# A column mean over 8192 x 8192: whole-tile first load, deeper input buffering, an uneven cast split, one PSUM accumulator and a piecewise last tile

## The chip, the cores and the metric

The kernel runs on one core of a Trainium2 chip. The metric is the device time of one execution in microseconds (us). Beside it stands the span, which the profiler takes from the first to the last instruction of one execution; here it is about 1.8 us shorter than the time.

Engines in the profile: PE is the matmul engine and PEld its weight loads, DVE the vector engine, ACT the scalar engine, SP the engine that issues the DMAs (SPq is its queue). A DMA has landed when all of its bytes are in. The PE clock is the share of full speed that was granted to PE.

## The reference

```python
x = np.random.randn(8192, 8192).astype(np.float32)
def reference(x):
    return np.mean(x, axis=0)          # 8192 column means
```

The input has 268.4 MB, the output 32 KB. Every input byte has to come in from HBM once, and little arithmetic is done on it.

## The kernel before

The rows are taken in 64 tiles of 128 rows (4.19 MB each). A tile t is loaded in f32, cast to f16 as th by ACT (left half) and DVE (right half), and PE sums over its 128 rows by a matmul whose weight is a column of 1/8192. The 16 column chunks of 512 go to eight PSUM banks, two rows in each. Three buffers hold t, three hold th.

```python
STREAM_BUFS = 3
CAST_BUFS = 3
SPLIT_FIRST_DMA = True
SPLIT_LAST_DMA = True
# ... (w0, w1: 128x2 weights, 1/R in one column, 0 in the other)
for i in range(n_tiles):
    t = stream.tile([P, C], f32, tag="t")
    th = casts.tile([P, C], f16, tag="th")
    src = x[i * P : (i + 1) * P, :]
    if first and SPLIT_FIRST_DMA:
        for r0 in range(0, P, 32):                      # four DMAs of 32 rows
            nc.sync.dma_start(out=t[r0 : r0 + 32, :], in_=src[r0 : r0 + 32, :])
    elif last and SPLIT_LAST_DMA:                       # two DMAs of half the columns
        nc.sync.dma_start(out=t[:, 0:half], in_=src[:, 0:half])
        nc.sync.dma_start(out=t[:, half:C], in_=src[:, half:C])
    else:
        nc.sync.dma_start(out=t, in_=src)
    if not last:
        nc.scalar.copy(out=th[:, 0:half], in_=t[:, 0:half])
        nc.vector.tensor_copy(out=th[:, half:C], in_=t[:, half:C])
        # ... 16 matmuls
        continue
    # ... last tile: casts, 16 matmuls, eight copies 2x512 from PSUM by DVE and ACT in turn
nc.sync.dma_start(out=out[0:half], in_=stage[0:1, 0:half])
nc.sync.dma_start(out=out[half:C], in_=stage[1:2, 0:half])
```

## Time and profile before

| | before |
|---|---|
| time, median | 646.23 us (646.15 to 646.82, 4 runs) |
| span of the profiled run | 644.4 us |
| first cast starts (tile 0 has landed) | 23.3 us |
| from the first cast of tile 0 to the last full tile's (62 periods) | 603.6 us |
| from there to the end (the tail) | 17.5 us |

The first view is the page of the kernel before: busy time of each engine with its share of the span, the DMA engines' busy tenths and the rate moved in 40 equal slices of 16.1 us, the chain of waits that ended last by engine, and the two casting groups (busy us, mean ns of one, then the idle time before them and what ended it).

```profile
PE 358.3 (56%) x1024; PEld 110.7 (17%) x1024; DVE 148.4 (23%) x72; ACT 236.0 (37%) x70; POOL 0.2 (0%) x4
...
DMA  9999999999999999999999999999999999999994
GB/s 197 350 429 423 430 443 427 427 431 438 427 429 435 430 428 429 441 425 429 426 443 429 426 431 436 429 431 435 429 430 429 437 429 430 427 437 433 427 424 182
...
DMA 85%; ACT 12%; PE 1%; DVE 0%; SPq 0%; issue 0%; ACTq 0%; DVEq 0%
...
L78 ACT CAST th<-t 128x4096 f16<-128x4096 f32 x63 | 227.1, 3605 | 378.8 <-DMA t<-in_x_dram 360.4
L79 DVE CAST th<-t 128x4096 f16<-128x4096 f32 x63 | 144.5, 2294 | 483.7 <-DMA t<-in_x_dram 461.5
```

No compute engine is busy for more than 56% of the span, the chain is 85% DMA, and both casts spend their idle time waiting for t. This is a kernel bound by its input stream. But the two rows of slices disagree at the left edge: the DMA engines count as busy there, while the rate is 197 and 350 GB/s instead of about 430. So the busy share alone does not tell at what rate a DMA engine moves bytes. Windows of 5 us over the start make it plain (columns: window and its length, busy time and count on PE, PEld, DVE, ACT, POOL, then the PE clock, the DMA share and GB/s):

```profile
0.00:5.00 5.00, 0.00 (x0) 0.08 (x1) 0.15 (x4) 0.00 (x0) 0.20 (x4) 1.00 0.94 210
5.00:10.00 5.00, 0.00 (x0) 0.00 (x0) 0.00 (x0) 0.00 (x0) 0.00 (x0) 1.00 1.02 210
...
15.00:20.00 5.00, 0.00 (x0) 0.00 (x0) 0.00 (x0) 0.00 (x0) 0.00 (x0) 1.00 1.02 210
```

For 20 us the rate is 210 GB/s at a DMA share of about one. The DVE timeline shows what it costs (start, duration, engine, line, operation; in brackets the idle time before it and what ended it):

```profile
23.33 2.29 DVE L79 CAST th<-t 128x4096 f16<-128x4096 f32 x1 [22.38 <-DMA t<-in_x_dram]
32.95 2.29 DVE L79 CAST th<-t 128x4096 f16<-128x4096 f32 x1 [7.33 <-DMA t<-in_x_dram]
42.66 2.29 DVE L79 CAST th<-t 128x4096 f16<-128x4096 f32 x1 [7.41 <-DMA t<-in_x_dram]
```

Tile 0 takes 23.3 us to arrive, tile 1 only 9.6 us more, and from there the casts start 9.71 us apart, which is 4.19 MB / 9.71 us = 432 GB/s.

The other end is the tail, after the last full tile is in (timeline of the kernel before):

```profile
626.90 3.60 ACT L78 CAST th<-t 128x4096 f16<-128x4096 f32 x1 [6.11 <-DMA t<-in_x_dram]
...
630.55 7.04 PE L53 MATMUL psum_all<-th,w 128*2 128x512 f16 x24 [4.42 <-ACT th L78]
...
632.05 3.60 ACT L86 CAST th<-t 128x4096 f16<-128x4096 f32 x1 [1.54 <-DMA t<-in_x_dram]
...
636.78 1.90 ACT L89 CAST th<-t 128x2048 f16<-128x2048 f32 x1 [1.13 <-DMA t<-in_x_dram]
...
638.58 2.47 DVE L95 COPY stage<-psum_all 2x512 f32<-2x512 f32 x4 [0.47 <-PE psum_all L53]
...
641.48 0.25 SPq L100 DMA_DIRECT2D out_dram<-stage  x1
```

The second half of the last tile lands just before 636.78. Two casts, eight matmuls, eight small copies and two output DMAs follow, until the span ends at 644.4.

### The profile page before, as it was taken

How to read it: one execution, taken by the hardware profiler on the slowest of the kernel's cores; microseconds unless marked ns; L12 is line 12 of the kernel's file. 1: busy time of each engine (PE TensorE's matmuls, PEld its weight loads, DVE VectorE, ACT ScalarE, POOL GpSimd, SP SyncE). 2: the span in 40 equal slices, each digit the busy share in tenths (PEclk: the TensorE clock that was granted, in tenths of full speed). 3: DMA queues.
4: the chain of work that ended last, by engine and by line, in shares of the span. 5: the costliest groups of instructions: out<-in, count | busy, mean ns of one | idle time of the engine just before them, and what ended most of it. 6: DMA issues, size and time to landing. Idle time of an engine off the chain costs nothing.

```text
span 644.4 us, 2618 instructions
## 1 busy us (share of the span) xinstructions
PE 358.3 (56%) x1024; PEld 110.7 (17%) x1024; DVE 148.4 (23%) x72; ACT 236.0 (37%) x70; POOL 0.2 (0%) x4
## 2 busy tenths in 40 slices
PE   0256746547547546566457456556556466466455
PEld 0011211112112112112112112112112112111111
DVE  0122121221221221221221221221221221221222
ACT  0343342442442442442432432433433433433436
POOL 0000000000000000000000000000000000000000
PEclk9986678876786687677776886786677766876888
DMA  9999999999999999999999999999999999999994
GB/s 197 350 429 423 430 443 427 427 431 438 427 429 435 430 428 429 441 425 429 426 443 429 426 431 436 429 431 435 429 430 429 437 429 430 427 437 433 427 424 182
DMA packets 9425, 268.64 MB, mean 417 GB/s; under 512 B 1090, under 2 KB 1090, under 8 KB 1090
## 3 DMA queue, kind: packets, MB, share of 16 engines
q1 hardware_dynamic: 9412, 268.47, 98.5%
q8 instruction: 8, 0.13, 0.1%
q14 instruction: 5, 0.04, 0.0%
HBM read 268.44 MB, written 0.03 MB: 417 GB/s over the span
## 4 chain that ended last, share of the span: by engine, by line
DMA 85%; ACT 12%; PE 1%; DVE 0%; SPq 0%; issue 0%; ACTq 0%; DVEq 0%
DMA t<-in_x_dram 85%; ACT th L78 12%; PE psum_all L53 1%; DVE stage L95 0%; SPq L70 0%; DVE th L90 0%; ACTq L78 0%; DVEq L126 0%; SPq L75 0%; SPq L72 0%; DVEq L90 0%
## 5 line engine op out<-in xcount | busy, mean ns | idle before, releaser
L53 PE MATMUL psum_all<-th,w 128*2 128x512 f16 x1024 | 358.3, 527 | 281.7 <-ACT th L78 281.2
L78 ACT CAST th<-t 128x4096 f16<-128x4096 f32 x63 | 227.1, 3605 | 378.8 <-DMA t<-in_x_dram 360.4
L79 DVE CAST th<-t 128x4096 f16<-128x4096 f32 x63 | 144.5, 2294 | 483.7 <-DMA t<-in_x_dram 461.5
L53 PEld LDWEIGHTS <-w 128*2 128x2 f16 x1024 | 110.7, 108 | 528.8 <-issue 484.6
L78 ACT ACT_TABLE_LOAD x1 | 1.3, 1283 | 23.3 <-DMA t<-in_x_dram 23.3
L86 ACT CAST th<-t 128x4096 f16<-128x4096 f32 x1 | 3.6, 3604 | 1.5 <-DMA t<-in_x_dram 1.5
L90 DVE CAST th<-t 128x2048 f16<-128x2048 f32 x1 | 1.2, 1226 | 7.7 <-DMA t<-in_x_dram 7.7
L95 DVE COPY stage<-psum_all 2x512 f32<-2x512 f32 x4 | 2.5, 672 | 0.5 <-PE psum_all L53 0.5
L89 ACT CAST th<-t 128x2048 f16<-128x2048 f32 x1 | 1.9, 1899 | 1.1 <-DMA t<-in_x_dram 1.1
L97 ACT COPY stage<-psum_all 2x512 f32<-2x512 f32 x4 | 2.1, 572 | 0.2
L41 DVE MEMSET w<- 128x1 f16 x1 | 0.1, 59 | 0.8 <-PEq L115 0.8
L115 POOL MEMSET const-bfloat16-1.0<- 128x1 bf16 x1 | 0.1, 102 | 0.0
L115 POOL MEMSET const-uint8-127<- 128x1 uint8 x1 | 0.1, 102 | 0.0
L115 POOL MEMSET const-float32-0.0<- 128x1 f32 x1 | 0.1, 99 | 0.2 <-issue 0.2
L115 POOL MEMSET const-float32-1.0<- 128x1 f32 x1 | 0.1, 99 | 0.0
L42 DVE MEMSET w<- 128x1 f16 x1 | 0.1, 59 | 0.0
L44 DVE MEMSET w<- 128x1 f16 x1 | 0.1, 59 | 0.0
L45 DVE MEMSET w<- 128x1 f16 x1 | 0.1, 59 | 0.0
## 6 DMA issues: line engine op xcount, KB each, us to landing
t<-in_x_dram SPq DMA_DIRECT2D x62, 4096.0 KB, 25.4
t<-in_x_dram SPq DMA_DIRECT2D x4, 1024.0 KB, 14.4
t<-in_x_dram SPq DMA_DIRECT2D x2, 2048.0 KB, 23.1
out_dram<-stage SPq DMA_DIRECT2D x2, 16.0 KB
```

The source lines that it names most:

```text
L41: nc.vector.memset(w0[:, 0:1], inv)
L42: nc.vector.memset(w0[:, 1:2], 0.0)
L44: nc.vector.memset(w1[:, 0:1], 0.0)
L53: nc.tensor.matmul(out=psum_all[0:2, b * 512 : (b + 1) * 512], lhsT=ws[m], rhs=th[:, j : j + 512], start=start, stop=stop,)
L78: nc.scalar.copy(out=th[:, 0:half], in_=t[:, 0:half])
L79: nc.vector.tensor_copy(out=th[:, half:C], in_=t[:, half:C])
L86: nc.scalar.copy(out=th[:, 0:half], in_=t[:, 0:half])
L89: nc.scalar.copy(out=th[:, half : half + qtr], in_=t[:, half : half + qtr])
L90: nc.vector.tensor_copy(out=th[:, half + qtr : C], in_=t[:, half + qtr : C])
L95: nc.vector.tensor_copy(out=stage[sl], in_=psum_all[sl])
L97: nc.scalar.copy(out=stage[sl], in_=psum_all[sl])
L115: nc = _bacc.Bacc("TRN2", target_bir_lowering=False, num_devices=1)
```

## The change

It is a retuning of the whole kernel: the first tile comes in one DMA of 128 rows; four stream buffers and two cast buffers instead of three and three; ACT casts 6 of the 16 column chunks and DVE 10; each chunk c has its own 128x16 weight with 1/8192 in column c, so all 1024 matmuls accumulate into one 16x512 region of one bank; the last tile comes in pieces of 5, 5, 5 and 1 chunks and is cast chunk by chunk; one copy and one output DMA end it. (A branch with REBAL_ROWS is switched off by its zero.)

```diff
-STREAM_BUFS = 3
-CAST_BUFS = 3
-SPLIT_FIRST_DMA = True
-SPLIT_LAST_DMA = True
+STREAM_BUFS = 4
+CAST_BUFS = 2
+ACT_CHUNKS = 6
+REBAL_TILE = 30
+REBAL_ROWS = 0
+PIECE_CHUNKS = (5, 5, 5, 1)
 ...
+    wall = consts.tile([P, n_chunk * n_chunk], f16)
+    nc.vector.memset(wall, 0.0)
+    for c in range(n_chunk):
+        nc.vector.memset(wall[:, c * n_chunk + c : c * n_chunk + c + 1], inv)
 ...
         nc.tensor.matmul(
-            out=psum_all[0:2, b * 512 : (b + 1) * 512],
-            lhsT=ws[m],
-            rhs=th[:, j : j + 512],
+            out=acc[0:n_chunk, :],
+            lhsT=wall[:, c * n_chunk : (c + 1) * n_chunk],
+            rhs=th[0:P, c * chunk : (c + 1) * chunk],
 ...
-        if first and SPLIT_FIRST_DMA:
-            for r0 in range(0, P, 32):
-                nc.sync.dma_start(out=t[r0 : r0 + 32, :], in_=src[r0 : r0 + 32, :])
+            nc.sync.dma_start(out=t[:, :], in_=x[r0 : r0 + P, :])
+        cast(t, th, 0, ACT_CHUNKS, on_act=True)
+        cast(t, th, ACT_CHUNKS, n_chunk, on_act=False)
+        for c in range(n_chunk):
+            mm(th, c)
 ... (last tile)
+    for cpp in PIECE_CHUNKS:
+        nc.sync.dma_start(out=t[:, c0 * chunk : (c0 + cpp) * chunk], in_=...)
+        for k in range(cpp):
+            cast(t, th, c0 + k, c0 + k + 1, on_act=(k < cpp // 2))
+        for k in range(cpp):
+            mm(th, c0 + k, stop=...)
+        c0 += cpp
 ...
+    nc.vector.tensor_copy(out=stage[:, :], in_=acc[0:n_chunk, :])
+    nc.sync.dma_start(out=out_v, in_=stage[:, :])
```

More of the change, by code (lines that the diff above doesn't have):

```diff
@@ L25 @@
     R, C = x.shape
-    assert R % P == 0
-    n_tiles = R // P
-    inv = 1.0 / float(R)
-    n_bank = (C + 1023) // 1024
-    assert n_bank <= 8 and C == n_bank * 1024
-    half = C // 2
-    qtr = half // 2
+    n_chunk = 16
+    chunk = C // n_chunk
+    n_bank = n_chunk // 2
+    assert C == 8192 and R % P == 0
+    inv = 1.0 / float(R)
+    n_tiles = R // P
+    assert sum(PIECE_CHUNKS) == n_chunk
     stream = ctx.enter_context(tc.tile_pool(name="stream", bufs=STREAM_BUFS))
@@ L38 @@
     psum = ctx.enter_context(tc.tile_pool(name="psum", bufs=1, space=bass.MemoryType.PSUM))
-    w0 = consts.tile([P, 2], f16)
-    nc.vector.memset(w0[:, 0:1], inv)
-    nc.vector.memset(w0[:, 1:2], 0.0)
-    w1 = consts.tile([P, 2], f16)
-    nc.vector.memset(w1[:, 0:1], 0.0)
-    nc.vector.memset(w1[:, 1:2], inv)
-    ws = (w0, w1)
-    stage = consts.tile([2, half], f32)
-    psum_all = psum.tile([P, 512 * n_bank], f32)
-    def mm(th, m, b, start, stop):
-        j = m * half + b * 512
+    wall = consts.tile([P, n_chunk * n_chunk], f16)
@@ L53, in mm @@
+    nc.vector.memset(wall, 0.0)
+    for c in range(n_chunk):
+        nc.vector.memset(wall[:, c * n_chunk + c : c * n_chunk + c + 1], inv)
+    stage = consts.tile([n_chunk, chunk], f32)
+    acc = psum.tile([P, chunk], f32)
+    out_v = out.rearrange("(c j) -> c j", j=chunk)
+    started = [False]
+    def mm(th, c, stop=False):
+        st = not started[0]
+        started[0] = True
         nc.tensor.matmul(
-            out=psum_all[0:2, b * 512 : (b + 1) * 512],
-            lhsT=ws[m],
@@ L56, in mm, with cast @@
-            rhs=th[:, j : j + 512],
-            start=start,
+            out=acc[0:n_chunk, :],
+            lhsT=wall[:, c * n_chunk : (c + 1) * n_chunk],
+            rhs=th[0:P, c * chunk : (c + 1) * chunk],
+            start=st,
             stop=stop,
         )
-    for i in range(n_tiles):
-        first = i == 0
-        last = i == n_tiles - 1
+    def cast(t, th, c0, c1, on_act):
+        sl = (slice(0, P), slice(c0 * chunk, c1 * chunk))
+        if on_act:
+            nc.scalar.copy(out=th[sl], in_=t[sl])
+        else:
+            nc.vector.tensor_copy(out=th[sl], in_=t[sl])
@@ L64 @@
+    for i in range(n_tiles - 1):
+        r0 = i * P
         t = stream.tile([P, C], f32, tag="t")
         th = casts.tile([P, C], f16, tag="th")
-        src = x[i * P : (i + 1) * P, :]
-        if first and SPLIT_FIRST_DMA:
-            for r0 in range(0, P, 32):
-                nc.sync.dma_start(out=t[r0 : r0 + 32, :], in_=src[r0 : r0 + 32, :])
-        elif last and SPLIT_LAST_DMA:
-            nc.sync.dma_start(out=t[:, 0:half], in_=src[:, 0:half])
-            nc.sync.dma_start(out=t[:, half:C], in_=src[:, half:C])
-        else:
-            nc.sync.dma_start(out=t, in_=src)
@@ L77 @@
-        if not last:
-            nc.scalar.copy(out=th[:, 0:half], in_=t[:, 0:half])
-            nc.vector.tensor_copy(out=th[:, half:C], in_=t[:, half:C])
-            for b in range(n_bank):
-                mm(th, 0, b, first, False)
-            for b in range(n_bank):
-                mm(th, 1, b, False, False)
-            continue
-        nc.scalar.copy(out=th[:, 0:half], in_=t[:, 0:half])
-        for b in range(n_bank):
-            mm(th, 0, b, first, False)
-        nc.scalar.copy(out=th[:, half : half + qtr], in_=t[:, half : half + qtr])
@@ L90 @@
-        nc.vector.tensor_copy(out=th[:, half + qtr : C], in_=t[:, half + qtr : C])
-        for b in range(n_bank):
-            mm(th, 1, b, False, True)
-            sl = (slice(0, 2), slice(b * 512, (b + 1) * 512))
-            if b % 2 == 0:
-                nc.vector.tensor_copy(out=stage[sl], in_=psum_all[sl])
-            else:
-                nc.scalar.copy(out=stage[sl], in_=psum_all[sl])
-    nc.sync.dma_start(out=out[0:half], in_=stage[0:1, 0:half])
-    nc.sync.dma_start(out=out[half:C], in_=stage[1:2, 0:half])
+        if i == REBAL_TILE and REBAL_ROWS:
+            q = REBAL_ROWS
+            nc.scalar.dma_start(out=t[0:q, :], in_=x[r0 : r0 + q, :])
+            nc.scalar.dma_start(out=t[q:P, :], in_=x[r0 + q : r0 + P, :])
+        else:
+            nc.sync.dma_start(out=t[:, :], in_=x[r0 : r0 + P, :])
@@ new lines @@
+        cast(t, th, 0, ACT_CHUNKS, on_act=True)
+        cast(t, th, ACT_CHUNKS, n_chunk, on_act=False)
+        for c in range(n_chunk):
+            mm(th, c)
+    r0 = (n_tiles - 1) * P
+    src = x[r0 : r0 + P, :]
+    t = stream.tile([P, C], f32, tag="t")
+    th = casts.tile([P, C], f16, tag="th")
+    c0 = 0
+    for cpp in PIECE_CHUNKS:
+        nc.sync.dma_start(
+            out=t[:, c0 * chunk : (c0 + cpp) * chunk],
+            in_=src[:, c0 * chunk : (c0 + cpp) * chunk],
+        )
+        for k in range(cpp):
+            cast(t, th, c0 + k, c0 + k + 1, on_act=(k < cpp // 2))
+        for k in range(cpp):
+            c = c0 + k
+            mm(th, c, stop=c == n_chunk - 1)
+        c0 += cpp
```

## The prediction

> **What bounds it now.** The input stream. The page's 40 slices show the DMA engines 9 tenths busy or more in every slice but the last, PE 56%, ACT 37%, DVE 23%; the chain of waits is 85% DMA of t and 12% ACT cast (the cast is only the link that frees a stream buffer; two other tiles are queued meanwhile). In the timeline the DVE casts start 9.71 us apart, 4.19 MB each, 432 GB/s. [...] So in steady state neither a fourth stream buffer, nor the 6/10 cast split, nor one PSUM accumulator can gain anything.
>
> **Where time is left.** (a) Start. The first cast waits until 23.3 us, but tile 1 follows only 9.65 us later. Windows of 1 us show zeros near 5, 10, 15 and 20 us: each of the four 32-row pieces of tile 0 takes about 5.05 us for 1 MB, 208 GB/s, though the slices call the engines busy. [...] half rate, as measured. (b) Tail. The last half tile lands at 636.76; two casts, 8 matmuls, eight 2x512 copies and two output DMAs follow until 644.4: 7.6 us.
>
> **What the change does.**
> - First tile as one 128-row DMA: 20.2 us of transfer becomes 9.7, so the first casts start at about 12.8 us instead of 23.3. On the critical path: -10.5 us (estimate from the above).
> - Middle: 62 periods unchanged. The cast becomes 2.7 us ACT / 2.9 DVE (estimate, scaling 3.605 us for 4096 columns on ACT, 2.294 on DVE) instead of 3.6. Off the path: 0. PE: the same 1024 matmuls of 512 columns, at most 6.8 us a tile[...]. CAST_BUFS 2 is enough: cast plus matmuls end 9.7 us after landing, the buffer is wanted after 19.4.
> - Last tile in 5/5/5/1 chunks: the last piece lands about 0.6 us after the third. The third piece's casts hold DVE about 1.4 us, then the last cast 0.43 (estimates from 2.29 and 1.23 us for 4096 and 2048 columns), then matmuls, one 16x512 copy (0.67) and one output DMA instead of two. I expect 5.8 us (full clock) to 6.8 us (half clock) after the last landing, instead of 7.6: -0.9 to -1.8. [...]
> - Seventeen memsets on idle DVE in the first 2 us: 0.
>
> **Sum.** 646.2 - 10.5 - 1.4 + 0.2 = 634.5; I say 634.2 us, range 632.6 to 636.2. The 2% line is at about 633.4, so it is close: faster 0.33, same 0.65, slower 0.02.
>
> **What shows each step.** First cast near 12.8 us, second about 9.7 later; the first two slices (197 and 350 GB/s) become near 400 and 430. Cast period stays 9.71. ACT busy falls to about 180 us and DVE rises to about 190, with no gain from it. From last landing to end about 6 us. PE busy about the same.
>
> **What would make it wrong.** The half-rate start may be a cold start and not the row split: then the first cast stays late and the time is near 644. Accumulating every matmul into one bank could stall PE enough to hold cast buffers: the waits view would show DVE waiting for PE and the period over 9.71. [...] One period of 10.98 us (near 80 us) is a hiccup of 1.3 us that may come or not.

The sum came to 634.5 us, and its -10.5 and -1.4 stand above with where they come from. Its + 0.2 is a guess for the narrow pieces; without it the sum is 634.3. That no buffer, split or accumulator could gain in steady state rests on the DMA's share alone (85% of the chain of waits, 90% busy or more in all slices but the last); that the stream could not be faster was not shown. The 6.8 us of matmuls a tile are an estimate from the trace before: in its slow stretches the weight loads start 0.43 us apart, and 16 matmuls took 6.50 us.

## More of the kernel before

Every run quoted was in the fast state. A program on one core has no second die to compare with, so only the spread of its own runs can show that.

## The result, and the profile after

The changed kernel took 633.91 us (median of 8 runs, 633.58 to 634.49), the kernel before 646.35 us in the same rounds (13 runs, 646.07 to 646.82). The ratio is 0.9808, with a 95% interval of 0.9798 to 0.9818: 1.9% faster, with the line of 2% inside the interval. All ratios here are the mean time of one kernel's fast runs over that of the other's fast runs of the same rounds, so they are not quite the ratio of the medians.

The span fell by 644.4 - 632.2 = 12.2 us. Read from the DVE timelines, it divides so:

| stretch | before | after | difference | predicted |
|---|---|---|---|---|
| start, to the first cast | 23.33 | 13.02 | -10.3 | -10.5 |
| first cast to the last full tile's, 62 periods | 603.6 | 604.2 | +0.6 | 0 |
| tail, from there to the end | 17.5 | 15.0 | -2.5 | -1.4 + 0.2 |

The page after (engines, and the rate in the 40 slices):

```profile
PE 360.0 (57%) x1024; PEld 118.6 (19%) x1024; DVE 182.9 (29%) x91; ACT 178.1 (28%) x70; POOL 0.2 (0%) x4
...
GB/s 373 433 437 431 432 431 433 433 431 430 432 433 431 432 428 433 431 431 431 428 433 431 431 432 430 431 435 431 431 430 431 431 433 430 431 431 430 431 418 234
```

The two slow slices have gone (373 and 433 GB/s). ACT lost 58 us of busy time and DVE gained 34; as the stream is the limit, this shows nowhere in the middle. The windows over the start:

```profile
0.00:5.00 5.00, 0.00 (x0) 0.09 (x1) 0.49 (x17) 1.28 (x1) 0.20 (x4) 1.00 0.69 242
5.00:10.00 5.00, 0.00 (x0) 0.00 (x0) 0.00 (x0) 0.00 (x0) 0.00 (x0) 1.00 1.05 452
```

The DVE timeline over the start:

```profile
13.02 2.83 DVE L69 CAST th<-t 128x5120 f16<-128x5120 f32 x1 [11.62 <-DMA t<-in_x_dram]
22.71 2.83 DVE L69 CAST th<-t 128x5120 f16<-128x5120 f32 x1 [6.87 <-DMA t<-in_x_dram]
```

The first tile is in at 13.0 us, and the next follows 9.7 us later as before. The +0.6 us in the middle is a few odd periods (one of 11.24 us at tile 6, where the kernel before had 10.98, and one of 10.09 near the end); in the other runs the same stretch took from 603.7 to 604.4 us, so no part of the change can be read from it (a_rows32_tile30, which slows the stream there on purpose, and a_earlype, whose last cast is cut, are left out).

The tail after:

```profile
617.18 2.75 ACT L67 CAST th<-t 128x3072 f16<-128x3072 f32 x1 [6.98 <-DMA t<-in_x_dram]
...
619.99 8.79 PE L56 MATMUL acc<-th,wall 128*16 128x512 f16 x32 [4.43 <-ACT th L67]
...
626.35 1.14 ACT L67 CAST th<-t 128x512 f16<-128x512 f32 x2 [1.94 <-DMA t<-in_x_dram]
626.35 1.43 DVE L69 CAST th<-t 128x512 f16<-128x512 f32 x4 [1.98 <-DMA t<-in_x_dram]
...
628.82 0.68 DVE L103 COPY stage<-acc 16x512 f32<-16x512 f32 x1 [1.03 <-PE acc L56]
629.52 0.36 SPq L104 DMA_DIRECT2D out_dram<-stage  x1
```

The line to look at is the second one. PE ran 32 matmuls as one unbroken group, all of the last full tile's and all of the last tile's, and the final copy waited for the end of it. The clock granted to PE moved during that group (windows after; the PE clock is the third number from the end):

```profile
620.00:622.00 2.00, 2.00 (x7) 0.72 (x7) 1.12 (x4) 1.14 (x2) 0.00 (x0) 0.65 1.00 420
622.00:624.00 2.00, 2.00 (x6) 0.59 (x5) 0.73 (x3) 0.73 (x2) 0.00 (x0) 0.50 0.98 409
624.00:626.00 2.00, 2.00 (x11) 0.82 (x10) 0.37 (x2) 0.41 (x1) 0.00 (x0) 1.00 0.60 236
626.00:628.80 2.80, 2.78 (x13) 0.97 (x11) 1.43 (x4) 1.14 (x2) 0.00 (x0) 1.00 0.02 6
```

In two windows of 2 us with a clock of 0.65 and 0.50 there are 7 and 6 matmuls, in the next one at 1.00 there are 11. Finer windows of this trace (0.1 us) put the half clock at 620.6 to 624.0 us, 3.4 us long.

How much this matters shows in seven profiled runs whose code from the last full tile on is the same (the changed kernel and six experiments of the next section that alter only how tile 0 or tile 30 is loaded):

| profiled runs | half clock around the group | group of 32 matmuls | tail |
|---|---|---|---|
| changed kernel, a_rows32, a_rows64, a_cols4 | 3.3 to 3.4 us | 8.8 us | 14.8 to 15.0 us |
| a_rows64_mid, a_rows32_strided, a_rows32_tile30 | 6.7 to 6.8 us | 9.9 to 10.0 us | 15.9 to 16.1 us |

The pages show it more coarsely: the clock of the last of the 40 slices is 8 tenths in the first four and 7 tenths in the other three.

Where the half clock is twice as long, the group and the tail are about 1.1 us longer with the same code. Tails of different kernels have to be compared at the same length of half clock, and the -2.5 us of the table above belongs to the short one (in the kernel before it was 3.4 us too). No run here tells what sets its length.

### The profile page after: what moved, and what is told of

The parts are those of the page before. It is cut to its first block, busy times and chain, and to the rows that moved or that the text cites. A ratio compares the mean times of both kernels' runs of the same rounds, so it can differ in the third digit from the quotient of the medians.

```text
span 632.2 us, 2631 instructions
## 1 busy us (share of the span) xinstructions
PE 360.0 (57%) x1024; PEld 118.6 (19%) x1024; DVE 182.9 (29%) x91; ACT 178.1 (28%) x70; POOL 0.2 (0%) x4
## 4 chain that ended last, share of the span: by engine, by line
DMA 90%; DVE 7%; PE 1%; ACT 0%; issue 0%; SPq 0%; DVEq 0%; ACTq 0%
DMA t<-in_x_dram 90%; DVE th L69 7%; PE acc L56 1%; ACT th L67 0%; SPq L80 0%; DVEq L69 0%; DVE stage L103 0%; ACTq L67 0%
## 5 line engine op out<-in xcount | busy, mean ns | idle before, releaser
L56 PE MATMUL acc<-th,wall 128*16 128x512 f16 x1024 | 360.0, 529 | 268.7 <-ACT th L67 268.7
L69 DVE CAST th<-t 128x5120 f16<-128x5120 f32 (+1 forms) x73 | 181.7, 2497 | 444.7 <-DMA t<-in_x_dram 444.7
L67 ACT CAST th<-t 128x3072 f16<-128x3072 f32 (+1 forms) x69 | 176.8, 2566 | 448.7 <-DMA t<-in_x_dram 448.7
L56 PEld LDWEIGHTS <-wall 128*16 128x16 f16 x1024 | 118.6, 116 | 509.7 <-issue 467.6
## 6 DMA issues: line engine op xcount, KB each, us to landing
t<-in_x_dram SPq DMA_DIRECT2D x1, 256.0 KB, 34.7
```

Source lines behind the costliest of these rows:

```text
L56: nc.tensor.matmul(out=acc[0:n_chunk, :], lhsT=wall[:, c * n_chunk : (c + 1) * n_chunk], rhs=th[0:P, c * chunk : (c + 1) * chunk], start=s ...
L67: nc.scalar.copy(out=th[sl], in_=t[sl])
L69: nc.vector.tensor_copy(out=th[sl], in_=t[sl])
```

## The experiments

Twelve kernels ran, all with a correct result. Those from "b_nosplit" to "a_rows32_tile30" ask why the start was slow, the others what the middle and the tail were worth. The first changes the kernel before, all others the changed kernel.

### b_nosplit: only the row split taken away

```diff
-SPLIT_FIRST_DMA = True
+SPLIT_FIRST_DMA = False
```

> The kernel before with only the row split of its first tile taken away. Partition theory (a 32-row DMA [...] runs at half rate): first cast near 13.0 us instead of 23.3, time about 646.3 - 10.3 = 636.0 us. Rival, cold start (the stream is slow at first whatever its form): first cast stays near 23 us, time about 646.

By the partition theory the expectations mean that the rate of a load depends on which partitions it writes. From the trace before it had two numbers: 1 MB into 32 rows took 5.05 us (208 GB/s), 4.19 MB into 128 rows 9.71 us (432 GB/s).

It took 636.57 us (ratio 0.9852, 0.9837 to 0.9866). Its first DVE cast in the timeline:

```profile
12.96 2.29 DVE L79 CAST th<-t 128x4096 f16<-128x4096 f32 x1 [12.01 <-DMA t<-in_x_dram]
```

The cold start is refuted: the same stream in the same place starts at full rate when it isn't cut by rows. One flag of the kernel before gives 9.8 us of the 12.4. The profiled run of this kernel had a PE clock of 0.594 on average (0.753 to 0.757 in its other runs), and its tail was 19.0 us instead of 17.5, at a clock of 0.62 from the last full tile's landing to 632.4 us (0.88 over the same work in the kernel before); it was the slowest of its four runs (637.54 against 636.19 to 636.67). The reading of the start does not depend on it.

### a_rows32: the row split put back into the changed kernel

```diff
-nc.sync.dma_start(out=t[:, :], in_=x[r0 : r0 + P, :])          # tile 0
+for q in range(0, P, 32):
+    nc.sync.dma_start(out=t[q : q + 32, :], in_=x[r0 + q : r0 + q + 32, :])
```

> The changed kernel with the old row split of tile 0 (four DMAs of 32 rows) put back. If the start is an additive 10.3 us of stream time: 633.9 + 10.3 = 644.2 us, first cast near 23.3 us. If the fourth stream buffer hides part of it: clearly less than 644.

It took 644.09 us (ratio 0.9968), with the first cast at 23.28 us:

```profile
23.28 2.83 DVE L69 CAST th<-t 128x5120 f16<-128x5120 f32 x1 [21.89 <-DMA t<-in_x_dram]
```

The cost is additive, 10.2 us added here and 9.8 us taken away from the kernel before, and the fourth buffer hides nothing of it: with the stream as the limit, the time lost to it wasn't made up.

### a_rows64 and a_rows64_mid: two DMAs against three

That 64 rows at 0..63 load as slowly as 32 rows, and 64 rows at 32..95 at the full rate, was the author's assumption; no trace had shown it before these runs. Two kernels were made in which it and a fixed cost per DMA predict opposite orders.

```diff
 # a_rows64, tile 0
+for q in range(0, P, 64):
+    nc.sync.dma_start(out=t[q : q + 64, :], in_=x[r0 + q : r0 + q + 64, :])
 # a_rows64_mid, tile 0
+for lo, hi in ((32, 96), (0, 32), (96, P)):
+    nc.sync.dma_start(out=t[lo:hi, :], in_=x[r0 + lo : r0 + hi, :])
```

> Tile 0 as two DMAs of 64 rows (0..63, 64..127). Partition theory[...]: still half rate, first cast near 23 us, about 644.2 us. Rival, a fixed cost per DMA of about 2.6 us (10.3 us over four DMAs): half as many, first cast near 18 us, about 639 us.

> Tile 0 as three DMAs: rows 32..95, then 0..31, then 96..127. Partition theory: [...] its 2 MB take about 4.9 us at full rate, and the two 32-row pieces about 5.1 us each at half rate: first cast near 13.0 + 5.2 = 18.2 us, about 639.1 us, FASTER than the two-DMA version although there is one DMA more. Rival, fixed cost per DMA: slower than the two-DMA version, by some 2.6 us.

They took 644.29 us (ratio 0.9969) and 639.73 us (ratio 0.9895). The version with one DMA more was 4.6 us faster. First the loads of tile 0 of a_rows64, by source line (duration of the issue; below, from issue to landing), then those of a_rows64_mid:

```profile
L81 SPq DMA_DIRECT2D t<-in_x_dram x2: 572/574/575, 0.7 to 1.4; - x2
...
DMA to landing us min/median/max: 13.1/17.7/22.4
```

```profile
L81 SPq DMA_DIRECT2D t<-in_x_dram x3: 421/561/640, 0.7 to 2.0; - x3
...
DMA to landing us min/median/max: 8.1/12.2/16.4
```

The first 2 MB took 13.1 us from issue to landing on rows 0..63, and 8.1 us on rows 32..95: same size, same form, 5.0 us apart, while 2.1 MB at 432 GB/s take 4.9 us. So the first was written at half rate, the second at full rate. (In a_rows64 the issues start at 0.7 and 1.4 us, so rows 64..127 landed 10.0 us after rows 0..63: 210 GB/s.) The first casts, a_rows64 and then a_rows64_mid:

```profile
23.87 2.83 DVE L69 CAST th<-t 128x5120 f16<-128x5120 f32 x1 [22.48 <-DMA t<-in_x_dram]
```

```profile
18.57 2.83 DVE L69 CAST th<-t 128x5120 f16<-128x5120 f32 x1 [17.17 <-DMA t<-in_x_dram]
```

A fixed cost per DMA is refuted, and the assumption held for both ranges. The runs show which partitions load at which rate; they do not show why.

### a_cols4 and a_rows32_strided: four DMAs of 1 MB spread over all partitions

```diff
 # a_cols4, tile 0
+for q in range(0, C, C // 4):
+    nc.sync.dma_start(out=t[:, q : q + C // 4], in_=x[r0 : r0 + P, q : q + C // 4])
 # a_rows32_strided, tile 0 (any row may go to any partition: it is a mean over rows)
+for q in range(4):
+    nc.sync.dma_start(out=t[q:P:4, :], in_=x[r0 + 32 * q : r0 + 32 * q + 32, :])
```

> Tile 0 as four DMAs of the same 1 MB as in a_rows32, but cut by columns, each over all 128 rows. Partition theory: full rate, first cast near 13.0 us, time about 634 us, the same as the changed kernel. Rival, four smaller DMAs cost 10.3 us whatever their form: about 644 us.

> Tile 0 as four DMAs of 32 rows each, same source rows and sizes as a_rows32, but written to every fourth partition (0,4,..124, then 1,5,..125, and so on). [...] about 634 us, first cast near 13 us. [...] in between, up to 644 us.

The two times in the second expectation are its two outcomes: 634 us if 32 partitions spread over the 128 load at full rate, more, up to 644, if they do not.

They took 634.20 us (ratio 0.9812) and 634.43 us (ratio 0.9813), the same as the changed kernel within their spreads. The first casts, a_cols4 and then a_rows32_strided:

```profile
13.02 2.83 DVE L69 CAST th<-t 128x5120 f16<-128x5120 f32 x1 [11.62 <-DMA t<-in_x_dram]
```

```profile
13.38 2.83 DVE L69 CAST th<-t 128x5120 f16<-128x5120 f32 x1 [11.98 <-DMA t<-in_x_dram]
```

The strided kernel reads the same 32 rows per DMA as a_rows32 and moves the same bytes in as many DMAs; only the partitions written differ, and 9.9 us of first-cast time go. That settles it: neither cutting the tile nor cutting it by rows was the trouble, but that each cut was a contiguous block of 32 partitions. The strided first cast is 0.36 us later than that of a_cols4, but kernels that load tile 0 in one DMA had theirs anywhere from 12.86 to 13.32 us, so nothing can be read from that.

### a_rows32_tile30: the split in mid stream

```diff
-nc.sync.dma_start(out=t[:, :], in_=x[r0 : r0 + P, :])          # tile 30
+for q in range(0, P, 32):
+    nc.sync.dma_start(out=t[q : q + 32, :], in_=x[r0 + q : r0 + q + 32, :])
```

> The row split of four 32-row DMAs moved from tile 0 to tile 30, in mid stream. Partition theory: same cost there, about 633.9 + 10.3 = 644.2 us, and one cast period of about 20 us. Rival, the row split costs only while the stream starts up, or queued tiles of the 4 buffers hide it: about 634 us.

It took 647.23 us (ratio 1.0013): 13.3 us more than the changed kernel, and more than the 10.3 expected. The DVE timeline around it:

```profile
286.45 2.83 DVE L69 CAST th<-t 128x5120 f16<-128x5120 f32 x1 [6.89 <-DMA t<-in_x_dram]
299.24 2.83 DVE L69 CAST th<-t 128x5120 f16<-128x5120 f32 x1 [9.96 <-DMA t<-in_x_dram]
318.95 2.83 DVE L69 CAST th<-t 128x5120 f16<-128x5120 f32 x1 [16.88 <-DMA t<-in_x_dram]
328.37 2.83 DVE L69 CAST th<-t 128x5120 f16<-128x5120 f32 x1 [6.59 <-DMA t<-in_x_dram]
```

The windows inside it and one after it:

```profile
300.00:305.00 5.00, 2.98 (x8) 0.95 (x8) 2.06 (x1) 1.97 (x1) 0.00 (x0) 0.50 0.98 210
305.00:310.00 5.00, 3.31 (x10) 1.05 (x9) 0.00 (x0) 0.00 (x0) 0.00 (x0) 0.75 0.99 206
...
325.00:330.00 5.00, 1.69 (x8) 0.63 (x7) 1.63 (x1) 1.65 (x1) 0.00 (x0) 1.00 1.01 433
```

The half rate is the same as at the start (206 to 210 GB/s). So the loss is a property of the DMA's form, not of the start. The 3.0 us too many are to be seen in the tile before: tile 29 came in 12.79 us after tile 28 instead of 9.71, and only then follows the period of 19.71. The stream thus lost about 12.8 us. My guess is that the first 32-row piece was already under way, at its lower rate, while tile 29 was not complete. The trace neither shows nor excludes this: the rate was 454 GB/s from 286.4 to 294.0 us and 139 GB/s from there to 299.2, so it fell about 5 us before tile 29 was complete, but the 0.72 MB moved in those 5 us are about what tile 29 still lacked (0.75 MB). No run tests it, and it stays open.

### a_oldmiddle and a_act8: the buffers and the cast split

```diff
 # a_oldmiddle                     # a_act8
-STREAM_BUFS = 4
+STREAM_BUFS = 3
-CAST_BUFS = 2
+CAST_BUFS = 3
-ACT_CHUNKS = 6                    -ACT_CHUNKS = 6
+ACT_CHUNKS = 8                    +ACT_CHUNKS = 8
```

> The changed kernel with the old middle: 3 stream buffers, 3 cast buffers, casts cut 8/8 instead of 6/10. If the middle is bound by the stream alone: the same as the changed kernel, 633.9 us within 0.4. If the fourth buffer or the shorter cast carries some of the gain: slower by over 1 us.

> Only the cast split of the changed kernel put back to 8/8; 4 stream and 2 cast buffers stay. Theory: PE carries the tail, 32 matmuls in a row from tile 63 of 64 on, and with 8/8 their first one waits 3.6 us for the ACT cast instead of 2.75: the same as with the whole old middle, about 635.5 us (0.9 us from the later start, the rest from the clock granted to PE there). Rival, the buffers made the difference: 633.9 us.

a_oldmiddle took 635.67 us (ratio 0.9833, runs 635.38 to 635.86), 1.8 us slower than the changed kernel: my expectation of "the same within 0.4" failed. Its middle stretch was 604.1 us, as in the changed kernel (604.2), but its tail was 16.6 us instead of 15.0. So a_act8 put back the cast split alone and took 635.27 us (ratio 0.9830, runs 634.98 to 636.07). By the medians the split carries 1.4 of the 1.8 us; what is left for the buffers, 0.4 us, lies within the spread of the runs. The tail of a_act8:

```profile
617.51 4.64 ACT L67 CAST th<-t 128x4096 f16<-128x4096 f32 x3 [6.12 <-DMA t<-in_x_dram]
...
621.17 8.59 PE L56 MATMUL acc<-th,wall 128*16 128x512 f16 x32 [3.15 <-ACT th L67]
...
629.79 0.68 DVE L103 COPY stage<-acc 16x512 f32<-16x512 f32 x1 [1.69 <-PE acc L56]
```

With 8 chunks on ACT, the cast of the last full tile takes 3.6 us instead of 2.75 (the line above shows it merged with the first two small casts), the group of 32 matmuls starts 3.7 us after the landing instead of 2.8, and the copy starts 12.3 us after it instead of 11.6. The profiled runs thus show 0.7 of the 1.4 us in the tail, and here the clock can be kept apart: a_act8 had the short half clock (3.3 us) and a tail of 15.7 us, against 14.8 to 15.0 us with the same half clock above; a_oldmiddle had the long one (6.8 us) and 16.6 us, against 15.9 to 16.1. At a like clock the split costs 0.5 to 0.9 us, and of the 1.6 us between the tails of a_oldmiddle and of the changed kernel about 1 us is the clock. The rest of the 1.4 us between the medians is not placed by a trace.

### a_pieces88 and a_pieces7531: the cuts of the last tile

```diff
-PIECE_CHUNKS = (5, 5, 5, 1)
+PIECE_CHUNKS = (8, 8)             # a_pieces88
+PIECE_CHUNKS = (7, 5, 3, 1)       # a_pieces7531
```

> The last tile in two pieces of 8 chunks instead of 5/5/5/1. After the last landing come four ACT casts (about 2.4 us), then five matmuls, copy and output: about 6.9 us from last landing to end instead of 5.3, so about 635.4 us. If the pieces carry the whole tail gain of about 2.4 us, it is 636.3; if none, 633.9.

> Tapered pieces, 7/5/3/1 chunks: piece three has two DVE casts instead of three, and PE has fewer matmuls queued when the last chunk lands. In the changed kernel the final copy begins 1.9 us after the last landing; here I expect about 1.0, so about 633.0 us, if the casts and matmuls of piece three were what the last chunk waited for. If the last landing and the output DMA alone set the tail: 633.9, no change.

a_pieces88 took 635.22 us (ratio 0.9827), near the 635.4 expected: the finer pieces are worth 1.3 us. a_pieces7531 took 634.09 us (ratio 0.9809), no gain where 0.9 us had been expected. Its tail shows why:

```profile
619.77 9.50 PE L56 MATMUL acc<-th,wall 128*16 128x512 f16 x32 [4.24 <-ACT th L67]
...
629.31 0.68 DVE L103 COPY stage<-acc 16x512 f32<-16x512 f32 x1 [2.09 <-PE acc L56]
```

The last casts were done at 627.2 by the same timeline, but PE was still working through its group of 32 matmuls, which took 9.50 us here (8.79 in the changed kernel), at a mean PE clock of 0.72 during the group (0.81 in the changed kernel's). This trace is of an odd run, the slowest of the four: its mean clock was 0.681 (0.753 to 0.759 in the others), and outside its half clock of 3.4 us its tail had 0.85 and not 1.00. So the 9.50 us are in part that clock. The median of the four runs still shows no gain; that the queue of PE is the reason is tested by the next kernel.

### a_earlype: start PE sooner

The last full tile is cast in three parts on each engine, so PE begins after the first part instead of after the whole cast; the last tile is cut 7/5/3/1.

```diff
+if i == n_tiles - 2:
+    for a0, a1, d0, d1 in ((0, 2, 6, 9), (2, 4, 9, 12), (4, 6, 12, 16)):
+        cast(t, th, a0, a1, on_act=True)
+        cast(t, th, d0, d1, on_act=False)
+        for c in (*range(a0, a1), *range(d0, d1)):
+            mm(th, c)
+    continue
```

> The changed kernel with PE started earlier in the tail: the last full tile is cast in three parts on each engine, so its matmuls begin about 1.0 us after the landing instead of 2.8, and the last tile is cut 7/5/3/1. If the 32 matmuls in a row set the tail: the final copy begins about 1.0 us after the last landing instead of 1.9, about 632.9 us. If PE is granted half clock through the tail, the gain is smaller, about 633.5. If casts and landings alone set it, as in 7/5/3/1 alone: 634.1.

It took 633.08 us (5 runs, 632.97 to 633.43; ratio 0.9795, 0.9781 to 0.9808), 0.8 us less than the changed kernel, and the two sets of runs do not overlap, although they come from different calls. It is the fastest of all kernels here. Its tail:

```profile
617.17 2.94 ACT L67 CAST th<-t 128x1024 f16<-128x1024 f32 x3 [6.97 <-DMA t<-in_x_dram]
...
618.27 3.61 PE L56 MATMUL acc<-th,wall 128*16 128x512 f16 x16 [2.77 <-ACT th L67]
...
627.03 1.02 PE L56 MATMUL acc<-th,wall 128*16 128x512 f16 x4 [0.33 <-ACT th L67]
...
628.10 0.68 DVE L110 COPY stage<-acc 16x512 f32<-16x512 f32 x1 [0.63 <-PE acc L56]
```

PE starts 1.1 us after the landing (618.27), the one group of 32 has come apart into several with waits between them, and the copy starts at 628.10, 10.9 us after the landing instead of 11.6. PE was granted full clock through the tail in the profiled run, and this is the only one of the fourteen traces in which it was. PE had been idle for 2.77 us before this tail, against 3.15 us (a_act8) to 4.43 us (the changed kernel) in the seven other traces where this was read. Whether the full clock comes from the earlier start is not shown: it is one trace, and the trial doesn't separate the two.

## Why the prediction was right

The predicted time was 634.2 us, in a range of 632.6 to 636.2, with "within 2%" as the likeliest outcome; the measured time is 633.91 us and the ratio 0.9808. That the point came so near is luck in part: the terms add up to 634.5, no term stands behind the step from there to 634.2, and two terms missed in opposite directions, the middle by +0.6 us and the tail by -1.3.

- **The bound: right.** Steady periods stayed at 9.71 us with the new buffers, split and accumulator: 4.19 MB in 9.71 us is 432 GB/s, as before. That this is the most that the stream can give was the author's assumption; no run tests it.
- **The start: right, in size and in the cause named, the row split.** Predicted -10.5 us, measured -10.3; first cast predicted at 12.8, measured 13.0. b_nosplit removed the rival named (cold start), and a_rows64_mid and a_rows32_strided the others.
- **The middle: right in the main.** The cast buffers, the single accumulator and the 16-column weights cost nothing that shows (PE busy 358.3 and 360.0 us). The +0.6 us came from odd periods that differ between the traces of the kernels (603.6 to 604.4 us, a_rows32_tile30 aside).
- **"Off the path: 0" for the cast split: wrong at the end.** It is right for 62 tiles and wrong for the last full one, where the end of the cast starts the last run of PE: a_act8 was 1.4 us slower by the medians and 0.7 to 0.9 us by the tails at a like clock.
- **The tail: direction right, size too small.** The sum had -1.4 + 0.2 = -1.2 us; the two traces show -2.5, at a like clock. The +0.2, a guess for narrow pieces, didn't show: the last piece landed 9.8 us after the last full tile, the second half before 9.9. From the last landing to the end 5.8 to 6.8 us were expected. The last piece was issued at 592.3 and landed 34.7 us later, at 627.0, which leaves 5.2 us. One term that was too large can be seen: the four last DVE casts were put at 1.4 + 0.43 us and took 1.43 us together. The split of the cast, counted as 0, is part of the rest. The sum also took PE as ready when the last piece landed. It was not, but this omission makes the tail longer and not shorter, so it offset a part of the error: how much of its 32 matmuls PE has left by then depends on when it began and what clock it got.
- **Not tested alone:** the single copy and the single output DMA in place of eight and two. The traces give a hint of their worth: in the trace before, the copies took 638.58 to 641.05 and the span ended 3.35 us after them; after it one copy of 0.68 us, and the end came 2.7 us after it.

## What to carry to other kernels

Cut a load so that every piece still covers all 128 partitions, or a set spread over them: cut by columns (first cast at 13.02 us here), or stride the partitions (13.38), and don't cut by blocks of 32 rows (23.28) or into the halves 0..63 and 64..127 (23.87); a busy DMA row in a profile does not show the loss (a share of about 1.0 at 210 and at 430 GB/s alike), the GB/s row does. In this kernel, bound by its stream, a microsecond lost to the stream at the start or in the middle was lost for good (10.2 us in a_rows32, 13.3 in a_rows32_tile30), while compute time cost only at the end (1.4 us in a_act8): look there for an engine with one unbroken group of work, and try to start it sooner (0.8 us here, with the clock not held apart). And before a difference of 1 us in a tail is explained by code, compare the PE clock of the two traces there.
